# Two-layer diffusion backbone: mixer C's keys and values projected first, from tiles not yet divided by the rms

## The chip, the cores and the metric

One core of a Trainium2 chip runs the whole program in one launch. The metric is the device time of that launch in microseconds (us), from a few executions of the same program. The engines named below are TensorE (PE, with its weight loads PEld), VectorE (DVE), ScalarE (ACT), GpSimd (POOL) and SyncE (SP). They run side by side, each takes its own instructions in order, and they meet through semaphores.

## What is computed

One inference step of a two-layer network over 384 tokens (128 context tokens and 256 latent tokens), model width 1024. Layer 0 mixes with a state space model and gated DeltaNet; layer 1 mixes with two kinds of attention (C and D). Each layer ends with a feed-forward block with a short convolution. The part that matters here is the entry of layer 1:

```python
h = _modulate(x, norm1_g, sh1, sc1)        # rms-norm, times g * (1 + sc1), plus sh1
proj = h @ w_in_cd                         # 1024 -> 2304 columns
qc, kc, vc, qd, kd, vd = split(proj)       # 512, 128, 128, 512, 512, 512
qc = _rms(qc per head of 64, c_qn); kc = _rms(kc per head, c_kn)
qd = _rms(qd per head, d_qn);       kd = _rms(kd per head, d_kn)
# latent tokens: q and k are rotated (rope2d); then attention C and D, output projection
x = x + g1 * out
x = x + g2 * ffn(_modulate(x, norm2_g, sh2, sc2))
```

Context tokens use one pair of shift and scale vectors, latent tokens another. `_rms(v, g)` is `v / sqrt(mean(v^2) + 1e-6) * g`.

## The kernel before

**Layout.** The residual stream `x` lies in 8 tiles of 128 features x 384 tokens. Every projection works in a split format: an operand is a high part (`ah` of an activation, `wh` of a weight) and a low part (`al`, `wl`), each of a reduced-precision 32-bit type, and a product is three matmuls: low x high, high x low, high x high. In layer 1's input projection (`block`) the activation tile is the stationary operand (128 features x 128 tokens, three chunks c of tokens), and the weights move (512 or 256 columns). A block of 512 columns is 8 features tiles x 3 chunks x 3 products = 72 matmuls into three PSUM banks.

**Weights.** `load_unit` (L266) brings 512 KB: SP loads the raw weights, ACT rounds them to `wh`. In layer 1 (`self.added`) ACT also writes the raw weights, negated and rounded, into `wl`, and POOL issues a second DMA that adds the raw weights onto them in SBUF (L277), so that the rest stays. There are four buffers for `wh` and `wl` and three for the raw tile. `w_in_cd` is 18 units in the order in which `block` takes them: queries of C (4 units of 512 columns), keys and values of C (2 units of 256 columns), then keys, queries and values of D (4 units each). The first four are preloaded.

**Entry of layer 1** (`layer_cd`, L1339). `norm_stats` (L1036) squares the 8 tiles on ACT, adds them on DVE, sums over features with matmuls against a column of ones (L1051), makes the reciprocal root r on DVE (`rsqrt`, 11 small instructions) and broadcasts r over the partitions with three more matmuls (L1059). `norm_mod` (L1063) then multiplies each tile by gain and r on DVE (L1077), adds the shift on ACT and rounds (`ah`, L1080), and takes the rest on DVE (`al`, L1081). `raw_mod` (L1086) is the variant of the feed-forward block: it makes the two parts from `x` times gain alone, without r and without the shift; there the shifts ride along as two more columns and r is multiplied in afterwards.

**PSUM.** In layer 1 there are three banks `mm` for a projection, two `sc`, two `pt` and one `po`. A new block needs each `mm` bank emptied by DVE (times the head gain, L1375) and ACT (square, L1377; for values a copy, L1425). The `ah` and `al` tiles have eight buffers each, so a ninth pair takes the place of the first.

**Order of the work.** The program text gives the dependences; the order in which each engine gets its instructions is made by a planner (`Order`, L1618). It gives every instruction a duration, follows the dependences, and lets each engine take, among what is ready, the instruction with the longest path behind it. A changed program is therefore planned anew as a whole.

Of the kernel before, what the change touches and what calls it, by code (L numbers as in the profile page):

```python
# [12 lines left out]
F32 = mybir.dt.float32  # L13
F32R = mybir.dt.float32r
I32 = mybir.dt.int32
AF = mybir.ActivationFunctionType
ALU = mybir.AluOpType
# [4 lines left out]
P = 128  # L22
D = 1024
KD = D // P
NCTX = 128
NLAT = 256
T = NCTX + NLAT
EPS = 1e-6
# [19 lines left out]
def _offsets(table):  # L48
# [14 lines left out]
    ("o16", 128), ("o32", 128), ("o64", 128), ("par", 8), ("npar", 8), ("ind", 16), ("dinit", 32),  # L63
    ("wm0", 128), ("wm1", 128), ("rcos", 2 * 32), ("rsin", 2 * 32),
]
# [14 lines left out]
def _consts():  # L80
    c = {}
    i = np.arange(P)
# [29 lines left out]
    c["wm0"] = np.where(i[None, :] <= i[:, None], 0.0, -1e30)  # L112
    c["wm1"] = np.where(i[:, None] <= i[None, :], 0.0, -1e30)
    comb = np.zeros((P, 8))
    for r in range(32):
# [27 lines left out]
def prep(inp):  # L143
# [50 lines left out]
    units = []  # L194
    for at, width in ((0, 512), (512, 256), (1280, 512), (768, 512), (1792, 512)):
        kk = 1024 // width
        blk = wc[:, at:at + width].reshape(KD // kk, kk, P, width).transpose(0, 2, 1, 3)
        units.append(blk.reshape(KD // kk, P, 1024))
# [18 lines left out]
class Trunk:  # L217
# [818 lines left out]
    def norm_stats(self, pool, tag="aux"):  # L1036
# [12 lines left out]
        for part in (sum_, sq):  # L1049
            for c in range(3):  # L1050
                nc.tensor.matmul(pss[:, c:c + 1], part[:, P * c:P * c + P], self.c("one"),  # L1051
                                 start=part is sum_ and c == 0, stop=part is sq and c == 2)
        ms = t(pool, [P, 3], "nms")
        v.tensor_scalar(ms, pss, 1.0 / D, EPS, ALU.mult, ALU.add)
        r = t(pool, [P, 3], "nr")
        self.rsqrt(pool, r, ms, "nrs")
# [28 lines left out]

    def raw_mod(self, pool, l, which):  # L1086

# [3 lines left out]
        part = 3 * which  # L1091
# [5 lines left out]
        for k in range(KD):  # L1097
            a, b = t(self.ap, [P, T + 2], "ah", F32R), t(self.ap, [P, T + 2], "al", F32R)
            sh = self.mod[l][:, 8 * part + k, :]
            nc.scalar.copy(a[:, T:], sh)  # L1100
            v.tensor_sub(b[:, T:], sh, a[:, T:].bitcast(F32))
            for c, s, e in SEGS:
                nc.scalar.mul(a[:, s:e], self.x[k][:, s:e], gs[:, k, c:c + 1])
                v.scalar_tensor_tensor(b[:, s:e], self.x[k][:, s:e], gs[:, k, c:c + 1], a[:, s:e].bitcast(F32),  # L1104
                                       ALU.mult, ALU.subtract)
            hh.append(a)
            hl.append(b)
# [231 lines left out]
    def layer_cd(self):  # L1339
# [3 lines left out]
        with tc.tile_pool(name="dpl", bufs=1, reuse_waits="tile") as pool:  # L1343
            pre = self.preload([I["w_in_cd"][n] for n in range(4)])
            hh, hl = self.norm_mod(pool, 1, 0, self.norm_stats(self.np, "pt"))
            ck, cv_ = t(pool, [P, P], "cck"), t(pool, [P, P], "ccv")
# [3 lines left out]
            lam = self.lambdas(pool)  # L1350
            nu = [0]

            def block(width):
# [14 lines left out]

            def normed(ps, nh, gain, tag):

                out = t(pool, [P, 3, nh, 64], tag)
                ss = t(pool, [P, 3, nh], "ass")
                for c in range(3):
# [4 lines left out]
                    v.tensor_reduce(ss[:, c], sq.rearrange("p (h d) -> p h d", d=64), AX.X, ALU.add)  # L1378
                v.tensor_scalar(ss, ss, 1.0 / 64, EPS, ALU.mult, ALU.add)
                r = t(pool, [P, 3, nh], "asr")  # L1380
# [35 lines left out]
            flat = lambda x: (lambda c: x[:, c].rearrange("p h d -> p (h d)"))  # L1416

            pq = block(512)
            qc = normed(pq, 8, self.s("cqn"), "aqc")
            qcT = to_features(flat(qc), 4, "aqT")  # L1420
            pkv = block(256)
            kc = normed(pkv, 2, self.s("ckn"), "akc")
            vc = t(pool, [P, 3, P], "avc")
            for c in range(3):
                nc.scalar.copy(vc[:, c, :], pkv[c][:, 128:256])  # L1425
            nc.sync.dma_start(self.O["new_ck"], kc[:, 0].rearrange("p h d -> p (h d)"))
# [519 lines left out]
```

## Time and profile before

| what | value |
|---|---|
| time, median of 3 runs | 1172.72 us (1171.16 to 1173.33) |
| the profiled execution's own time | 1167.5 us |
| its span, first to last instruction | 1165.7 us |
| PE busy | 1114.2 us, 96% of the span |
| DVE, ACT, POOL busy | 804.1, 607.0, 25.5 us |
| mean granted TensorE clock | 0.977 of full speed |
| feed-forward block 0 ends on PE | 683.6 us into the span |
| input projection of keys of D begins | 720.9 us |

The span leaves out what lies before the first and after the last instruction. Busy shares are means over stages with different limits; a stage is read from its own stretch. "Granted clock" 1.00 is 2.4 GHz, 0.50 is 1.2 GHz. PE rows give the start of an instruction and its time through the array; neighbours overlap, so the pace is the distance of their starts.

### The profile page before, as it was taken

What the parts mean: (1) busy time and instruction counts of PE and PEld (TensorE: products, weight loads), DVE (VectorE), ACT (ScalarE), POOL (GpSimd) and SP (SyncE); (2) the same over time, 40 slices, a digit from 0 to 9 for tenths busy, and PEclk for the clock granted to TensorE, in tenths of its full rate; (3) what the DMA queues carried; (4) which work ended last, traced back from release to release, by engine and by line L of the source; (5) the groups of instructions that cost most, each with busy time, mean ns of one, the idle gap of its engine ahead of it and who ended that gap; (6) DMA issues with size and microseconds to landing.
All of it is one profiled execution on the core that took longest, in us unless ns stands there. A gap on an engine that the chain in (4) does not pass through costs nothing.

```text
span 1165.7 us, 20343 instructions
## 1 busy us (share of the span) xinstructions
PE 1114.2 (96%) x7699; PEld 968.6 (83%) x7699; DVE 804.1 (69%) x2071; ACT 607.0 (52%) x1327; POOL 25.5 (2%) x41
## 2 busy tenths in 40 slices
PE   4899999999999999999999989999999999999998
PEld 1587676686558999999999978667699999999998
DVE  7987688789876868767753447574867877676332
ACT  5666364557545555555542346755655655554221
POOL 0000000000000000000000011011000000000000
PEclk8688998999999999999999989999999999999999
DMA  9343465446864233433334479666253343333541
GB/s 376 138 121 134 150 226 173 157 144 246 333 236 132 95 110 126 141 113 127 121 117 133 125 180 235 147 154 135 56 109 127 111 142 109 127 130 101 159 137 53
DMA packets 54482, 174.49 MB, mean 150 GB/s; under 512 B 8688, under 2 KB 12656, under 8 KB 54128
## 3 DMA queue, kind: packets, MB, share of 16 engines
q1 hardware_dynamic: 49200, 154.72, 39.5%
q0 software_dynamic: 3744, 13.63, 7.1%
q10 hardware_dynamic: 1440, 4.85, 1.1%
q8 instruction: 60, 0.98, 0.3%
q14 instruction: 38, 0.31, 0.1%
HBM read 170.16 MB, written 3.01 MB: 149 GB/s over the span
## 4 chain that ended last, share of the span: by engine, by line
PE 85%; DVE 7%; ACT 3%; DMA 2%; issue 1%; ACTq 0%; SPq 0%; DVEq 0%
PE mm L1127 16%; PE mm L1128 16%; PE mm L1126 16%; PE mod L1011 3%; PE mm L1364 2%; PE mm L1366 2%; PE mm L1365 2%; PE pj L1128 1%; PE sc L1486 1%; PE pj L1127 1%; PE pj L1126 1%; DVE xt L1158 1%; PE mq L1011 1%; PE mod L1126 1%; PE mod L1128 1%
## 5 line engine op out<-in xcount | busy, mean ns | idle before, releaser
L274 ACT CAST wh<-raw 128x1024 fp32r<-128x1024 f32 (+2 forms) x193 | 194.1, 1027 | 198.8 <-PE mm L1128 160.9
L279 DVE TENSOR_TENSOR wl<-raw,wh 128x1024 fp32r<-128x1024 f32 x167 | 195.5, 1191 | 109.3 <-ACT wh L274 109.3
L1126 PE MATMUL mm<-ah,wl 128*128 128x386 f32 (+1 forms) x732 | 234.0, 342 | 3.5 <-DVE xt L1158 2.0
L1127 PE MATMUL mm<-al,wh 128*128 128x386 f32 (+1 forms) x732 | 232.9, 340 | 1.9 <-DVE al L1104 1.4
L1128 PE MATMUL mm<-ah,wh 128*128 128x386 f32 (+1 forms) x732 | 232.7, 340 | 0.0
L1126 PEld LDWEIGHTS mm<-ah,wl 128*128 128x128 f32 x732 | 137.5, 190 | 5.4 <-issue 2.4
L1127 PEld LDWEIGHTS mm<-al,wh 128*128 128x128 f32 x732 | 137.6, 190 | 3.0 <-DVE al L1104 2.1
L1128 PEld LDWEIGHTS mm<-ah,wh 128*128 128x128 f32 x732 | 137.8, 190 | 0.0
L1128 PE MATMUL mm<-fgh,wh 128*128 128x384 f32 x352 | 107.2, 339 | 0.0
L1127 PE MATMUL mm<-fgl,wh 128*128 128x384 f32 x352 | 106.9, 338 | 0.0
L1126 PE MATMUL mm<-fgh,wl 128*128 128x384 f32 x352 | 106.8, 338 | 0.0
L1185 ACT ACTIVATE fz<-fz,fsh 128x128 f32<-128x128 f32 x88 | 35.6, 450 | 67.2 <-DVE fz L1182 67.2
L1126 PEld LDWEIGHTS mm<-fgh,wl 128*128 128x128 f32 x352 | 65.3, 188 | 0.0
L1127 PEld LDWEIGHTS mm<-fgl,wh 128*128 128x128 f32 x352 | 65.2, 188 | 0.0
L1128 PEld LDWEIGHTS mm<-fgh,wh 128*128 128x128 f32 x352 | 65.1, 188 | 0.0
L1158 DVE SCALAR_TENSOR_TENSOR xt<-mm,mod,xt 128x128 f32<-128x128 f32 (+1 forms) x38 | 14.1, 413 | 62.5 <-PE mm L1128 62.5
L1182 DVE TENSOR_TENSOR fz<-mm,nrb 128x384 f32<-128x384 f32 x88 | 45.9, 550 | 0.2
L1190 DVE SCALAR_TENSOR_TENSOR fy<-fz,sml,fy 128x127 f32<-128x127 f32 x88 | 36.4, 414 | 12.9 <-ACT fy L1188 12.1
L276 ACT ACTIVATE wl<-raw 128x1024 fp32r<-128x1024 f32 x26 | 27.5, 1059 | 28.2 <-PE mm L1365 22.7
L1126 PE MATMUL pj<-ah,wl 128*128 128x384 f32 x112 | 39.9, 358 | 2.1 <-DVE wl L279 2.1
L1197 DVE SCALAR_TENSOR_TENSOR fs<-fz,fsh,fs 128x128 f32<-128x128 f32 x88 | 32.7, 414 | 12.5 <-ACT fs L1195 11.2
L1128 PE MATMUL pj<-ah,wh 128*128 128x384 f32 x112 | 40.8, 364 | 0.0
(664 smaller groups left out, 2220.5 us busy)
## 6 DMA issues: line engine op xcount, KB each, us to landing
raw<-in_ffn_up_dram SPq DMA_DIRECT2D x88, 512.0 KB, 3.4
raw<-in_w_mod_dram SPq DMA_DIRECT2D x54, 512.0 KB, 4.7
raw<-in_ffn_down_dram SPq DMA_DIRECT2D x32, 512.0 KB, 4.4
wh<-in_w_mod_dram SPq DMA_DIRECT2D x21, 512.0 KB, 6.0
wl<-in_w_mod_dram SPq DMA_DIRECT2D x21, 512.0 KB, 6.1
raw<-in_w_in_ab_dram SPq DMA_DIRECT2D x20, 512.0 KB, 3.5
raw<-in_w_in_cd_dram SPq DMA_DIRECT2D x18, 512.0 KB, 5.6
wl<-in_w_in_cd_dram POOLq DMA_DIRECT2D x18, 512.0 KB, 7.1
```

Source lines behind the costliest of these rows:

```text
L274: nc.scalar.copy(wh[:, :cols], raw[:, :cols])
L276: nc.scalar.mul(wl[:, :cols], raw[:, :cols], -1.0)
L279: nc.vector.tensor_sub(wl[:, :cols], raw[:, :cols], wh[:, :cols].bitcast(F32))
L1011: nc.tensor.matmul(pr[32 * n:32 * n + 32], self.sc[:, k, 30 - 2 * b:62 - 2 * b], raws[n // 2][:, 512 * (n % 2):512 * (n % 2) + 512], start ...
L1126: nc.tensor.matmul(out, wl, xh, start=first, stop=False)
L1127: nc.tensor.matmul(out, wh, xl, start=False, stop=False)
L1128: nc.tensor.matmul(out, wh, xh, start=False, stop=last)
L1158: self.nc.vector.scalar_tensor_tensor(self.x[n][:, s:e], ps[:, s:e], self.m(l, gate, n, c), self.x[n][:, s:e], ALU.mult, ALU.add)
L1182: v.tensor_mul(z[i][0], ps[:, 0:T], rb)
L1185: nc.scalar.activation(pa[:, a:b], pa[:, a:b], AF.Identity, bias=sa[:, c:c + 1])
L1190: v.scalar_tensor_tensor(y[:, a + 1:b], pa[:, a:b - 1], w[:, 0:1], y[:, a + 1:b], ALU.mult, ALU.add)
L1197: v.scalar_tensor_tensor(s[:, a:b], pb[:, a:b], sb[:, c:c + 1], s[:, a:b], ALU.add, ALU.mult)
```

## The change

Keys and values of C become the first block of the input projection, and it no longer works on the normalised tiles. `raw_mod` makes tiles that hold `x` times gain only. Since the rms is one number per token, the projected rows are the wanted ones times the rms, except for the shift's part. That part is a row per token group: shift (two columns) times the same weights gives two rows, which are added as rms x row by one small product per token chunk. The keys are normalised per head, so the common factor drops out once the epsilon is scaled by the mean square; the values are multiplied by r. The other four blocks use normalised tiles as before. The weight units are stored in the new order.

```diff
-    ("wm0", 128), ("wm1", 128), ("rcos", 2 * 32), ("rsin", 2 * 32),
+    ("cond", 2), ("wm0", 128), ("wm1", 128), ("rcos", 2 * 32), ("rsin", 2 * 32),
...
+    c["cond"] = (i[:, None] % 32) == np.arange(2)[None, :]
...
-    for at, width in ((0, 512), (512, 256), (1280, 512), (768, 512), (1792, 512)):
+    for at, width in ((512, 256), (0, 512), (1280, 512), (768, 512), (1792, 512)):
...
-    def raw_mod(self, pool, l, which):
+    def raw_mod(self, pool, l, which, n=T + 2):
...
-            a, b = t(self.ap, [P, T + 2], "ah", F32R), t(self.ap, [P, T + 2], "al", F32R)
-            sh = self.mod[l][:, 8 * part + k, :]
-            nc.scalar.copy(a[:, T:], sh)
-            v.tensor_sub(b[:, T:], sh, a[:, T:].bitcast(F32))
+            a, b = t(self.ap, [P, n], "ah", F32R), t(self.ap, [P, n], "al", F32R)
+            if n > T:
+                sh = self.mod[l][:, 8 * part + k, :]
+                nc.scalar.copy(a[:, T:], sh)
+                v.tensor_sub(b[:, T:], sh, a[:, T:].bitcast(F32))
...
             pre = self.preload([I["w_in_cd"][n] for n in range(4)])
-            hh, hl = self.norm_mod(pool, 1, 0, self.norm_stats(self.np, "pt"))
+            raw = self.raw_mod(self.np, 1, 0, T)
+            sh, sl_ = t(pool, [P, KD, 2], "ash", F32R), t(pool, [P, KD, 2], "asl", F32R)
+            nc.scalar.copy(sh, self.mod[1][:, 0:KD, :])
+            v.tensor_sub(sl_, self.mod[1][:, 0:KD, :], sh.bitcast(F32))
+            norm = self.norm_stats(self.np, "pt")
+            rms, inv = t(pool, [P, 3], "arms"), self.r
+            v.tensor_mul(rms, self.ms, inv)
+            eps = t(pool, [P, 3], "aeps")
+            v.tensor_scalar(eps, self.ms, EPS, None, ALU.mult)
+            hh, hl = self.norm_mod(pool, 1, 0, norm)
...
+            def raw_block():
+                (rh, rl), width, kk = raw, 256, 4
+                ps = [self.mm([P, width]) for _ in range(3)]
+                pw = self.bank("po", [2, width])
+                for u in range(2):
+                    wh, wl = pre[u]
+                    for c in range(3):
+                        for i in range(kk):
+                            k = kk * u + i
+                            sl, ts_ = slice(width * i, width * i + width), slice(P * c, P * c + P)
+                            nc.tensor.matmul(ps[c], rl[k][:, ts_], wh[:, sl], start=k == 0, stop=False)
+                            nc.tensor.matmul(ps[c], rh[k][:, ts_], wh[:, sl], start=False, stop=False)
+                            nc.tensor.matmul(ps[c], rh[k][:, ts_], wl[:, sl], start=False, stop=False)
+                    for i in range(kk):
+                        sl = slice(width * i, width * i + width)
+                        k = kk * u + i
+                        self.mm3(pw, (sh[:, k], sl_[:, k]), (wh[:, sl], wl[:, sl]), k == 0, k == KD - 1)
+                nu[0] = 2
+                rows = t(pool, [2, width], "art4")
+                nc.scalar.copy(rows, pw)
+                pr = self.bank("pt", [2, 3, P])
+                for c in range(3):
+                    nc.tensor.matmul(pr[:, c, :], rms[:, c:c + 1].to_broadcast([P, 2]), ident, start=True, stop=True)
+                each = t(pool, [2, 3, P], "ado", bufs=2)
+                nc.scalar.mul(each[:, 0], pr[:, 0], self.c("cond")[0:2, 0:1])
+                nc.scalar.mul(each[:, 1:], pr[:, 1:], self.c("cond")[0:2, 1:2])
+                for c in range(3):
+                    nc.tensor.matmul(ps[c], each[:, c, :], rows, start=False, stop=True)
+                return ps
...
-                v.tensor_scalar(ss, ss, 1.0 / 64, EPS, ALU.mult, ALU.add)
+                if eps is None:
+                    v.tensor_scalar(ss, ss, 1.0 / 64, EPS, ALU.mult, ALU.add)
+                else:
+                    v.scalar_tensor_tensor(ss, ss, 1.0 / 64, eps.unsqueeze(2).to_broadcast([P, 3, nh]),
+                                           ALU.mult, ALU.add)
...
+            pkv = raw_block()
+            kc = normed(pkv, 2, self.s("ckn"), "akc", eps)
+            vc = t(pool, [P, 3, P], "avc")
+            for c in range(3):
+                nc.scalar.mul(vc[:, c, :], pkv[c][:, 128:256], inv[:, c:c + 1])
             pq = block(512)
             qc = normed(pq, 8, self.s("cqn"), "aqc")
             qcT = to_features(flat(qc), 4, "aqT")
-            pkv = block(256)
-            kc = normed(pkv, 2, self.s("ckn"), "akc")
-            vc = t(pool, [P, 3, P], "avc")
-            for c in range(3):
-                nc.scalar.copy(vc[:, c, :], pkv[c][:, 128:256])
```

## Rows read from the trace of the kernel before

**Rows 1.** The page's first part: busy time, share and instructions of each engine.

```profile
PE 1114.2 (96%) x7699; PEld 968.6 (83%) x7699; DVE 804.1 (69%) x2071; ACT 607.0 (52%) x1327; POOL 25.5 (2%) x41
```

**Rows 2.** Windows from 600 us: length, busy us per engine, clock, DMA share, GB/s.

```profile
core 0: us, PE busy (x) PEld busy (x) DVE busy (x) ACT busy (x) POOL busy (x), PEclk, DMA share, GB/s
600.00:676.00 76.00, 76.00 (x435) 76.00 (x434) 30.20 (x43) 23.16 (x29) 0.31 (x1) 1.00 0.43 134
684.00:688.00 4.00, 1.50 (x12) 1.42 (x12) 3.83 (x27) 4.00 (x6) 1.73 (x2) 1.00 0.40 70
688.00:692.00 4.00, 1.62 (x6) 1.36 (x6) 1.58 (x12) 2.53 (x4) 0.86 (x1) 0.61 1.04 211
692.00:696.00 4.00, 3.63 (x9) 2.59 (x10) 3.36 (x10) 1.61 (x4) 0.00 (x0) 0.54 1.02 289
696.00:700.00 4.00, 4.00 (x19) 3.27 (x18) 2.53 (x9) 3.04 (x6) 0.86 (x1) 1.00 1.05 323
700.00:720.00 20.00, 19.71 (x122) 17.38 (x120) 13.92 (x41) 13.46 (x20) 3.46 (x4) 1.00 0.97 226
720.00:884.00 164.00, 158.88 (x823) 115.71 (x824) 112.40 (x418) 101.50 (x237) 14.71 (x17) 1.00 0.56 129
```

**Rows 3.** Timeline of PE, 683 to 721 us: start, us, what, idle before and releaser.

```profile
683.41 0.33 PE L1128 MATMUL mm<-fgh,wh 128*128 128x384 f32 x1
685.18 0.83 PE L1051 MATMUL pt<-cst,nacc 128*128 128x1 f32 x6 [1.43 <-DVE nacc L1047]
...
689.49 1.62 PE L1059 MATMUL pt<-cst,nr 128*128 128x128 f32 x6 [2.81 <-DVE nr L294]
692.37 0.80 PE L1364 MATMUL mm<-wh,al 128*128 128x512 f32 x1 [1.26 <-DVE al L1081]
...
709.38 0.63 PE L1364 MATMUL mm<-wh,al 128*128 128x512 f32 x2
709.84 0.63 PE L1365 MATMUL mm<-wl,ah 128*128 128x512 f32 x2
...
710.78 0.28 PE L1364 MATMUL mm<-wh,al 128*128 128x256 f32 x1
...
719.33 0.38 PE L1410 MATMUL pt<-cst,aqc 128*128 128x128 f32 x2
720.89 0.74 PE L1364 MATMUL mm<-wh,al 128*128 128x512 f32 x2 [1.18 <-ACT avc L1425]
```

**Rows 4.** Timeline of PE at 114 us: 16-column stationary beside a full one.

```profile
114.52 0.34 PE L1126 MATMUL su<-ah,wl 128*16 128x384 f32 x1
114.69 0.34 PE L1126 MATMUL pj<-ah,wl 128*128 128x384 f32 x1
```

**Rows 5.** Timeline of PE: plain f32 products, 128 columns, then 256 columns, in pairs.

```profile
46.03 0.94 PE L1059 MATMUL sy<-cst,nr 128*128 128x128 f32 x6
...
747.12 1.08 PE L1509 MATMUL po<-acpt,avc 128*64 128x256 f32 x6
```

**Rows 6.** Raw tiles of feed-forward 1, by line: min/median/max ns, first and last start.

```profile
L1103 ACT ACTIVATE ah<-xt,ngs x16: 387/448/504, 872.5 to 881.3; 128x128 fp32r<-128x128 f32 x8, 128x256 fp32r<-128x256 f32 x8
L1104 DVE SCALAR_TENSOR_TENSOR al<-xt,ngs,ah x16: 349/421/492, 880.0 to 885.2; 128x128 fp32r<-128x128 f32 x8, 128x256 fp32r<-128x256 f32 x8
```

**Rows 7.** Timeline of DVE at 683 us: the last residual addition.

```profile
683.78 0.74 DVE L1158 SCALAR_TENSOR_TENSOR xt<-mm,mod,xt 128x128 f32<-128x128 f32 x2
```

**Rows 8.** Timeline of ACT, then of POOL: the second weight unit's low part.

```profile
683.52 0.53 ACT L1042 ACTIVATE nsq<-xt 128x384 f32<-128x384 f32 x1 [7.21 <-DVE xt L1158]
683.95 1.04 ACT L276 ACTIVATE wl<-raw 128x1024 fp32r<-128x1024 f32 x1
...
685.30 0.87 POOL L277 DMA_DIRECT2D wl<-in_w_in_cd_dram  x1 [8.60 <-DVE lmp L1454]
```

**Rows 9.** POOL's DMA issues at 675, 685 and 689 us: us to landing.

```profile
wl<-in_w_in_cd_dram POOLq DMA_DIRECT2D x1, 512.0 KB, 7.2
...
wl<-in_w_in_cd_dram POOLq DMA_DIRECT2D x1, 512.0 KB, 5.3
...
wl<-in_w_in_cd_dram POOLq DMA_DIRECT2D x1, 512.0 KB, 11.4
```

More of the change, by code (lines that the diff above doesn't have):

```diff
@@ L1052, in norm_stats @@
                                  start=part is sum_ and c == 0, stop=part is sq and c == 2)
-        ms = t(pool, [P, 3], "nms")
+        self.ms = ms = t(pool, [P, 3], "nms")
         v.tensor_scalar(ms, pss, 1.0 / D, EPS, ALU.mult, ALU.add)
-        r = t(pool, [P, 3], "nr")
+        self.r = r = t(pool, [P, 3], "nr")
         self.rsqrt(pool, r, ms, "nrs")
@@ L1367, in block, with normed @@
                 return ps
-            def normed(ps, nh, gain, tag):
+            def normed(ps, nh, gain, tag, eps=None):
                 out = t(pool, [P, 3, nh, 64], tag)
```

## Prediction

> **What bounds the kernel now.** I read the page's busy times first: PE is busy for 1114 of 1166 us, and no other engine comes near [rows 1]. So time can be won where PE stands still or runs slowly, and every matmul that is added costs its own time unless it falls into such a hole. Then I went through windows of the layer that the change touches. Before 684 us PE is full and DVE and ACT have more than half their time free; from 684 to 692 us PE works 3.1 of 8 us, and from 688 to 696 the granted clock is 0.61 and 0.54, so most of the time at the lower of its two levels, 1.2 GHz. From 696 us PE is full again at full clock, and from 720 to 884 us it lacks only 5.1 of 164 us [rows 2]. The hole at the entry of layer 1 is the only large one here.
>
> The timeline of PE gives its parts [rows 3]. The feed-forward block's last product starts at 683.41 us; at the pace of 0.18 us that stretch is over at 683.59. Then PE waits 1.43 us for the sum of squares, 2.81 us for the reciprocal root, 1.26 us for the first normalised tile, and after the keys and values 1.18 us for ACT to empty a bank. The first block of D starts at 720.89 us: 37.3 us after the feed-forward block.
>
> What would those 37.3 us hold without waits, at full clock? The sums of squares take 1.5 us (685.18 to 686.68, where the next idle time of 2.81 us begins). The broadcast of r takes 0.94 us at full clock (the same six records at 46 us [rows 5]; here they took 1.62 [rows 3]). The query block is 72 products at 0.23 us (two starts lie 0.46 apart [rows 3]), 16.6 us; it took 692.37 to 710.78, 18.4 us, because it began at the low clock. Keys and values are 72 products from 710.78 to 719.33, 8.55 us, or 0.119 each. Two transposes take some 0.25 us. The sum is 27.8, so 9.5 us of the 37.3 are lost: 6.7 idle, 0.7 and 1.8 at the low clock, 0.3 in the draining of the array.
>
> **What is removed.** The block of keys and values needs r only at its end, so it can fill the time in which PE now waits for r. Its tiles come from x alone. Seven of the eight x tiles are final before the last residual additions; the eighth is final at 684.5 [rows 7]. A raw tile is two ACT products of about 0.45 us and two DVE ones of about 0.42 [rows 6]. Most of the 32 run under the feed-forward block, where DVE is busy for 30 and ACT for 23 of 76 us [rows 2]; I take that as free. Only the last two tiles fall behind 683.5 us, about 1.8 us on ACT and 1.7 on DVE, side by side; they are features 6 and 7, needed in the second half of the block, some 6 us later. Without that cover the 16 products of ACT would be 7.2 us in front of the block.
>
> **What is added on PE.** The two shift rows are 24 products of 256 moving columns with a stationary operand of two columns. No row here has two columns; the nearest has 16, and it takes its full 0.175 us of the stream like its 128-column neighbour [rows 4]. So each is priced like a full one, 24 x 0.119 = 2.85 us; a price of nothing would need them to run beside others, and the 16-column ones did not. The broadcast of rms is three plain f32 products of 128 columns, 0.94 us as for r [rows 5]. The three last products are plain f32, two rows deep and 256 columns wide: doubling the 128-column row gives 1.7 us, the 256-column row gives 1.0 for six records that ran in pairs; I take 1.3. Together 5.1 us, between 4.8 and 5.5. The small DVE steps (rms, epsilon, low part of the shift) are under 0.2 us each and lie before the root or beside it. The value products with r replace copies one for one.
>
> **The new sequence.** At 683.6 PE can start the first half of the raw block: its low weights were issued at 675 us and took 7.2 us [rows 9], so they are there by 683. This half is 36 x 0.119 = 4.3 us, its shift rows 1.4, the sums of squares 1.5: work until 690.8. The root is ready at 689.3 (the moment at which the broadcast starts now, less a hand-over), which adds two broadcasts, 1.9 us. The second half needs the second unit's low weights. ACT makes their negative at 683.95, behind a square that waits for x, POOL issues the addition at 685.30 [rows 8], and it took 5.3 us [rows 9]: 690.6. So in the existing times nothing is late. The normalised tiles then take the buffers of the raw ones as these are used up, and about 1.75 us each on DVE (four operations of 0.35 to 0.48 us) against 2.1 us in which PE uses one up: from 691 on they are ahead of the query block, which begins near 699.
>
> The sum on PE is 27.8 + 5.1 = 32.9 us instead of 37.3, a gain of 4.4, less what still waits. The query block takes the three banks of the keys and values, which ACT and DVE must empty, and the same hand-over costs 1.18 us today at the other end of the block [rows 3]. The change moves it and does not remove it. That leaves 3.2 us. Behind this, PE has nearly no idle time up to 884 us [rows 2], so an earlier start is passed on. The profiled execution's 1167.5 us become 1164.3; the median of the runs shown stands 5.2 us above that execution, and the same difference from it gives **1169.5 us**. A difference under 0.2% (2.3 us) could not be told from no change.
>
> **Rivals.**
>
> *A second wait at the bank hand-over.* ACT serves squares, value products, weight casts and normalised tiles in one row. It is busy for 24.6 us between 684 and 720 [rows 2]; the change adds some 2.5 us there and wants it done 3 to 4 us earlier, so about 27 of 32.5. If two weight operations of 1.04 us [rows 8] stand before the square that frees a bank, the hand-over costs 3.3 instead of 1.2 and the gain is 1.1: 1171.6, no measurable change. For it speaks that today's hand-over already waits for ACT; against it that the planner can put the square first.
>
> *The second unit's weights are late, and the clock falls.* The DMA engines are full from 688 us on, and the addition issued at 689 us took 11.4 us instead of 5.3 [rows 2, 9]. With that duration the second unit lands at 696.7. PE then runs out of work at 692.6, waits 4.1 us, and starts at the low clock again, which today costs the query block 1.8 us. The sum is 4.4 - 1.2 - 4.1 - 1.8, 2.7 us slower: 1175.4. With the clock's part it decides against the change from a landing near 694 us, 8.7 us after the issue. For it speaks that the buffer of that unit is freed only when the feed-forward block ends; against it that the unit is the first of three additions and took 5.3 us. The Trainium skill ("TensorE: Matmul & The Clock Gate", section "HAM oscillation — how this bites in real kernels") says the same against such loops: an array that waits for a transfer inside them falls back to half rate and pays it again at the restart. The trace agrees on the fall, with 0.61 and 0.54 after the waits here [rows 2]. Another page speaks for the change: "DMA: Bandwidth & Descriptors" (the Trainium skill, section "Anatomy of one DMA — SWDGE (gpsimd) path") fits such a DMA with 2.0 us plus its bytes at 436 GB/s, an estimate of 3.2 us for 512 KB, by which this rival would be out; no addition in these rows is that short, and the rows decide.
>
> *More is won.* The hand-over is hidden behind the three last products (0), and the plan behind it closes 1.5 of the 5.1 us that PE lacks later, since keys of C are ready before the queries: 5.9 us, 1166.8. Against it: nothing in the rows shows that those later gaps hang on the keys.
>
> **How the numbers follow.** The forecast gets 0.50, with a range of its own from 1168 to 1171.3; of this about 0.10 lies within 0.2%. The hand-over rival gets 0.25, the late weights 0.15, the larger gain 0.10. So faster 0.40 + 0.10 = 0.50, no change 0.10 + 0.25 = 0.35, slower 0.15. The range goes from the larger gain, 1166.5, to just short of the late weights, 1175. The new plan of the whole program can move any of these by a microsecond or so, which is why the forecast's own range is as wide as it is.
>
> **What would show it.** Right: in the changed profile PE goes from the feed-forward block into products on 256 columns without a pause, the clock row stays at 1.00 through 684 to 700 us, the 24 shift products take about 0.12 us each, and the first block of D begins some 33 to 35 us after the feed-forward block. Wrong: an idle time of PE before the raw block's second half with a low clock after it; the bank hand-over above 2 us; raw tiles that stand in front of the weight casts under the feed-forward block, so that PE is no longer full before 684 us; or a gain at the entry that the attention stages give back as new gaps behind 720 us.

## The result, and the profile after

| | median | lowest to highest | runs |
|---|---|---|---|
| before | 1171.82 us | 1165.74 to 1174.80 | 20 |
| changed | 1176.43 us | 1171.61 to 1186.91 | 20 |

The ratio is 1.0053, 95% interval [1.0038, 1.0067]: the change made the kernel slower by 0.53%; the medians lie 4.6 us apart. The forecast of 1169.5 us had the wrong sign, and the time lies 1.4 us above its range.

The page's first part, of the changed kernel, against [rows 1]:

```profile
PE 1125.3 (96%) x7735; PEld 976.7 (83%) x7735; DVE 810.2 (69%) x2091; ACT 613.3 (52%) x1347; POOL 25.4 (2%) x41
```

PE is busy for 11 us more, with 36 more instructions. That is more than the added products cost: the mean granted clock of the profiled execution fell from 0.977 to 0.972, and PE counts as busy at the lower clock too.

Single executions differ in places that the change does not touch: around 404 us, in the first feed-forward block, where PE has the same instructions in the same order in both kernels, the profiled execution of the changed kernel ran 4 us at a granted clock of 0.59 and that of before did not. So the traces are compared over one stage: from the start of the first feed-forward block's last product (683.41 us before [rows 3], 686.13 after) to the first product of the second one. This stage took 195.53 us before and 200.70 after. The 5.2 us are in it. Each kernel has one traced execution, so a stage is one execution's, while the medians are of 6 to 20 executions.

The timeline of PE at the entry of layer 1, changed kernel (start, us, what, idle before and releaser), against [rows 3]:

```profile
686.13 0.33 PE L1130 MATMUL mm<-fgh,wh 128*128 128x384 f32 x1
687.65 0.35 PE L1376 MATMUL mm<-wh,al 128*128 128x256 f32 x1 [1.19 <-DVE al L1106]
...
700.15 0.83 PE L1060 MATMUL pt<-cst,nr 128*128 128x128 f32 x6
700.91 0.82 PE L1389 MATMUL pt<-cst,arms 128*2 128x128 f32 x6
701.66 0.28 PE L1130 MATMUL po<-wh,ash 128*2 128x256 f32 x1
702.43 1.56 PE L1394 MATMUL mm<-art,ado 2*128 2x256 f32 x6 [0.49 <-ACT art L1385]
704.84 0.62 PE L1408 MATMUL mm<-wh,al 128*128 128x512 f32 x1 [0.85 <-ACT avc L1470]
705.26 0.63 PE L1409 MATMUL mm<-wl,ah 128*128 128x512 f32 x1
```

The three long waits of before for the sum, the root and the first normalised tile (1.43, 2.81 and 1.26 us) are gone; 1.19, 0.49 and 0.85 us stand in their place. The last row is the new loss: a product of 512 columns starts 0.42 us after the one before, where the pace at full clock is 0.23. Windows of the changed kernel show the granted clock (last but two; columns as in [rows 2]):

```profile
688.00:704.00 16.00, 15.49 (x126) 13.57 (x124) 10.70 (x56) 9.15 (x16) 2.59 (x3) 1.00 0.99 259
704.00:706.00 2.00, 1.16 (x3) 0.96 (x4) 1.95 (x7) 1.98 (x7) 0.00 (x0) 0.77 1.00 188
706.00:708.00 2.00, 2.00 (x6) 1.52 (x6) 2.00 (x8) 1.33 (x4) 0.00 (x0) 0.50 0.97 292
708.00:710.00 2.00, 2.00 (x10) 1.61 (x9) 1.93 (x9) 0.80 (x2) 0.00 (x0) 0.88 0.11 34
...
744.00:746.00 2.00, 0.66 (x4) 0.54 (x5) 1.04 (x4) 1.99 (x5) 0.67 (x1) 1.00 0.56 104
746.00:748.00 2.00, 2.00 (x6) 1.16 (x5) 1.46 (x4) 2.00 (x8) 0.00 (x0) 0.51 1.02 180
748.00:750.00 2.00, 2.00 (x8) 1.49 (x7) 0.95 (x4) 0.77 (x3) 0.00 (x0) 0.64 0.84 240
```

As forecast the clock is 1.00 through the raw block. But it falls twice behind it, at the start of the query block and at 746 us. Summed over windows of 2 us, what the clock lacks to 1.00, times the length, is 3.4 us in this stage, and it was 3.4 before. The fall at the entry was not removed; it was moved and split.

The second fall lies where attention C begins. PE there, changed kernel:

```profile
738.10 0.82 PE L1458 MATMUL pt<-cst,aqc 128*128 128x128 f32 x6
...
739.93 0.49 PE L1458 MATMUL pt<-cst,akc 128*128 128x128 f32 x3
...
741.63 0.49 PE L1534 MATMUL sc<-akT,aqT 64*128 64x128 f32 x2
742.04 0.96 PE L1410 MATMUL mm<-wh,ah 128*128 128x512 f32 x3
742.93 0.48 PE L1534 MATMUL sc<-akS,aqT 64*128 64x128 f32 x2
745.34 0.48 PE L1534 MATMUL sc<-akT,aqT 64*128 64x128 f32 x2 [1.92 <-ACT acp L1547]
745.84 0.63 PE L1408 MATMUL mm<-wh,al 128*128 128x512 f32 x1
```

The keys of C, projected first, are transposed at 739.93, behind the last of the four query transposes. Their last rows were ready long before, as DVE shows:

```profile
722.00 0.22 DVE L1449 TENSOR_TENSOR akc<-art,art 128x64 f32<-128x64 f32 x1
```

The first scores follow at 741.63, 55.5 us into the stage against 48.7 before. D's key block, the work with which PE bridges such waits, begins 0.4 us earlier than before. So at the first score 69 of its 72 products have started, where before it were 41: three are left (742.04), then PE stands for 1.92 us and the clock falls. In the kernel before, the same wait of the scores for ACT is 0.41 us:

```profile
732.14 0.48 PE L1486 MATMUL sc<-akT,aqT 64*128 64x128 f32 x2
...
735.75 0.48 PE L1486 MATMUL sc<-akT,aqT 64*128 64x128 f32 x2 [0.41 <-ACT acp L1499]
```

TensorE's time in the stage, summed over starts by kind of product, divides the 5.2 us. Added products: 5.28 (shift 1.10, 0.94 and 0.93; broadcast of rms 0.75; last products 1.56). Idle time above 60 ns: 10.06 to 7.44, so -2.61. Broadcast of r, now at full clock: -0.86. The 512-column products: +1.57. Score products on half the array in C and D: +1.90. The sum is 5.3.

Of the 1.90, 0.31 is the low clock at 748 us. The other 1.59 comes from which score products the plan puts next to each other (a plain f32 product is two records). The last two of D, one for each half of the array, stand together before, and the next product starts 0.85 us after the first; after the change other work stands between them, and each takes 0.84 us. Before, then after:

```profile
850.42 0.92 PE L1546 MATMUL mm<-akdT,aqT 64*128 64x384 f32 x4
851.27 0.61 PE L1126 MATMUL sc<-ah,wl 128*128 128x384 f32 x2
...
856.08 0.91 PE L1594 MATMUL mm<-akdT,aqT 64*128 64x384 f32 x2
...
858.45 0.91 PE L1594 MATMUL mm<-akdT,aqT 64*128 64x384 f32 x2
```

That is 0.83 us. Two products of C on 384 columns stood together in the same way before (749.02 to 749.90) and do not after: 0.76 us.

### The profile page after: what moved, and what is told of

Same layout as the page of the kernel before. It is cut to its first block, busy times and chain, and to the rows that moved or that the text cites. A ratio compares the mean times of both kernels' runs of the same rounds, so it can differ in the third digit from the quotient of the medians.

```text
span 1174.6 us, 20451 instructions
## 1 busy us (share of the span) xinstructions
PE 1125.3 (96%) x7735; PEld 976.7 (83%) x7735; DVE 810.2 (69%) x2091; ACT 613.3 (52%) x1347; POOL 25.4 (2%) x41
## 4 chain that ended last, share of the span: by engine, by line
PE 87%; DVE 6%; ACT 3%; DMA 2%; issue 1%; ACTq 0%; SPq 0%; DVEq 0%
PE mm L1129 16%; PE mm L1130 16%; PE mm L1128 16%; PE mod L1012 3%; PE mm L1408 2%; PE mm L1409 2%; PE mm L1410 2%; PE sc L1534 1%; PE pj L1130 1%; PE pj L1129 1%; PE pj L1128 1%; PE mod L1128 1%; PE mm L1594 1%; PE mod L1130 1%; PE mod L1129 1%
## 5 line engine op out<-in xcount | busy, mean ns | idle before, releaser
L1130 PE MATMUL mm<-fgh,wh 128*128 128x384 f32 x352 | 103.5, 336 | 0.0
L1129 PE MATMUL mm<-fgl,wh 128*128 128x384 f32 x352 | 103.5, 336 | 0.0
L1128 PE MATMUL mm<-fgh,wl 128*128 128x384 f32 x352 | 103.2, 336 | 0.0
```

What stands on the lines that cost most here:

```text
L1128: nc.tensor.matmul(out, wl, xh, start=first, stop=False)
L1129: nc.tensor.matmul(out, wh, xl, start=False, stop=False)
L1130: nc.tensor.matmul(out, wh, xh, start=False, stop=last)
```

## The experiments

Each run is timed against before on its own chip (medians 1171.0 to 1171.8 us). The marks are starts on PE in the traced execution, in us into the stage.

| kernel | query block | D's keys | C's first scores | stage | median | ratio to before, interval |
|---|---|---|---|---|---|---|
| before | 8.95 | 37.48 | 48.73 | 195.53 | | |
| changed | 18.70 | 37.07 | 55.49 | 200.70 | 1176.43 | 1.0053 [1.0038, 1.0067] |
| order only | 23.94 | 40.69 | 59.29 | 207.68 | 1181.83 | 1.0112 [1.0076, 1.0148] |
| order, keys turned first | 23.97 | 41.05 | 55.61 | 200.41 | 1175.89 | 1.0030 [1.0015, 1.0046] |
| no shift | 14.12 | 33.28 | 51.63 | 196.84 | 1170.71 | 0.9999 [0.9983, 1.0016] |
| x in eight tiles | 18.30 | 36.92 | 55.60 | 201.35 | 1176.26 | 1.0050 [1.0025, 1.0075] |
| wide | 18.80 | 35.57 | 54.00 | 197.68 | 1173.83 | 1.0031 [1.0006, 1.0056] |
| shift alone wide | 18.90 | 37.28 | 55.98 | 201.19 | 1175.20 | 1.0033 [1.0014, 1.0052] |
| keys turned first | 18.71 | 37.16 | 51.72 | 196.51 | 1169.64 | 0.9989 [0.9972, 1.0006] |
| keys first, wide | 18.80 | 35.94 | 50.50 | 195.31 | 1170.51 | 1.0000 [0.9981, 1.0019] |
| keys first, wide, eight tiles | 18.33 | 35.47 | 50.03 | 195.41 | 1170.03 | 0.9990 [0.9973, 1.0006] |
| keys first, wide, four rows | 17.60 | 35.08 | 49.64 | 194.48 | 1167.45 | 0.9970 [0.9948, 0.9991] |
| turned block | 13.80 | 38.42 | 58.96 | 212.24 | 1179.26 | 1.0078 [1.0043, 1.0114] |
| turned, eight tiles, keys first | 15.38 | 38.59 | 55.22 | 201.41 | 1174.81 | 1.0036 [1.0021, 1.0052] |

**The order alone, on normalised tiles.**

```diff
-    for at, width in ((0, 512), (512, 256), (1280, 512), (768, 512), (1792, 512)):
+    for at, width in ((512, 256), (0, 512), (1280, 512), (768, 512), (1792, 512)):
...
+            pkv = block(256)
+            kc = normed(pkv, 2, self.s("ckn"), "akc")
...
             pq = block(512)
...
-            pkv = block(256)
...
```

> Only the order is changed: keys and values of C come first, but on normalised tiles, with no shift rows and no rms products. The stage is taken from the start of the last product of feed-forward 0 to the first of feed-forward 1: 195.5 us in the kernel before, 200.7 in the changed one. Theory A (the loss is the sum of 5.3 us of added products, two falls of the clock and a later start of attention C, against a hole that is only partly filled): order alone keeps the whole hole at the entry and adds the later start of attention C, some 2 to 3.5 us: stage 197.5 to 199. Theory B (the order alone makes the loss, since the long chain of the queries now starts last, and the added products lie in the hole): stage 200 or more, as slow as the changed kernel. If the order costs nothing, 195.5.

It lost 12 us in the stage: in theory B's range, and 7 us above the changed kernel. Its timeline of PE:

```profile
690.25 1.62 PE L1059 MATMUL pt<-cst,nr 128*128 128x128 f32 x6 [2.66 <-DVE nr L294]
693.13 0.58 PE L1364 MATMUL mm<-wh,al 128*128 128x256 f32 x1 [1.26 <-DVE al L1081]
...
694.58 0.79 PE L1364 MATMUL mm<-wh,al 128*128 128x256 f32 x2 [0.45 <-DVE al L1081]
```

and windows of it:

```profile
692.30:696.30 4.00, 2.72 (x11) 2.43 (x12) 2.94 (x9) 2.00 (x5) 0.00 (x0) 0.50 1.04 188
696.30:700.30 4.00, 4.00 (x21) 4.00 (x21) 3.37 (x11) 1.60 (x4) 0.00 (x0) 0.53 1.00 281
```

The entry's waits stay. The block behind them is half as wide and waits for four more tiles (0.45, then 1.25, 0.37 and 0.39 us), and the clock stays at 0.50 for longer than before [rows 2]. In this order the raw tiles are worth 7.0 us of the stage (207.68 to 200.70), and the new order takes more than that away.

**Without the shift.** This kernel leaves the shift out of C's keys and values: no shift products, no rms broadcast, no last products.

> The changed kernel without the shift's part of keys and values: the 24 two-column products, the broadcast of rms and the three two-row products are left out, so the keys and values lack the shift. Theory A: these products cost what they take on PE, 5.3 us, and if they also bring the fall of the clock at the query block, 1.8 us more: stage 195.4, or 193.6 with the clock. Theory B (they lie in the hole): stage within 1 us of 200.7.

3.9 of the 5.3 us came back. In front of the query block PE now waits longer:

```profile
699.37 0.47 PE L1392 MATMUL mm<-wh,al 128*128 128x512 f32 x1 [1.89 <-ACT avc L1454]
```

and the clock falls there (0.74, 0.50) and at the scores, as in the change. PE's idle time in the stage is 1.4 us longer than in the changed kernel: that part of the added work had lain in waits. So the added work alone doesn't explain the loss: without it the kernel only comes level with before.

**x in eight tiles.** The planner keeps an engine's reads of a tile behind that engine's own last write to it. DVE writes the residuals, so with x in one tile the low parts (DVE, L1106) all follow the last residual; ACT, which only reads x, makes its parts from 612 us on. DVE in the changed kernel shows it:

```profile
686.50 0.74 DVE L1160 SCALAR_TENSOR_TENSOR xt<-mm,mod,xt 128x128 f32<-128x128 f32 x2 [3.50 <-PE mm L1130]
687.16 0.74 DVE L1106 SCALAR_TENSOR_TENSOR al<-xt,ngs,ah 128x128 fp32r<-128x128 f32 x2
```

```diff
-    def load_x(self, pool):
+    def load_x(self, pool, apart=False):
+        if apart:
+            self.x = [self.t(pool, [P, T], f"xt{k}") for k in range(KD)]
...
```

> The changed kernel with the residual stream in eight tiles of their own instead of one, so that the planner may place the low parts of the raw tiles on DVE before the last residual addition. Theory E (the first raw product waits 1.2 us because the planner keeps all DVE reads of the one tile behind its last DVE write): the low parts of features 0 to 5 run under feed-forward 0, the wait of 1.2 us goes, the root of the rms comes some 3 us earlier, and the stage is 1.2 to 2 us shorter, 198.7 to 199.5; the same at the entry of feed-forward 1 takes another 1 to 2 us. Rival: the low parts stay late for another reason, stage 200.7.

The raw block starts at once in the trace of this run, and that is all:

```profile
680.63 0.34 PE L1130 MATMUL mm<-fgh,wh 128*128 128x384 f32 x1
680.81 0.40 PE L1381 MATMUL mm<-wh,al 128*128 128x256 f32 x2
681.89 0.36 PE L1381 MATMUL mm<-wh,al 128*128 128x256 f32 x1 [0.69 <-DVE xt L1160]
```

A wait of 0.69 us comes one step later, the query block starts 0.4 us earlier, and the stage is no shorter. This wait is real and not the cause.

**Wide operands.** The same number of products, with 128 stationary columns or rows in place of two, by slices of 128 columns of the shift tile and zero rows.

```diff
-                pw = self.bank("po", [2, width])
+                pw = self.bank("po", [P, width])
...
-                        self.mm3(pw, (sh[:, k], sl_[:, k]), (wh[:, sl], wl[:, sl]), k == 0, k == KD - 1)
+                        at = slice(2 * k, 2 * k + P)
+                        self.mm3(pw, (sh[:, at], sl_[:, at]), (wh[:, sl], wl[:, sl]), k == 0, k == KD - 1)
...
-                rows = t(pool, [2, width], "art4")
+                rows = t(pool, [P, width], "art4")
...
-                    nc.tensor.matmul(pr[:, c, :], rms[:, c:c + 1].to_broadcast([P, 2]), ident, start=True, stop=True)
+                    nc.tensor.matmul(pr[:, c, :], rms[:, c:c + 1].to_broadcast([P, P]), ident, start=True, stop=True)
```

> The changed kernel, with the same number of products and the same columns streamed, but the shift products and the rms broadcast use a stationary operand of 128 columns, and the last three products are 128 rows deep (all rows but two are zero). Theory C (the clock falls at the start of the query block because PE just ran narrow products): the granted clock stays at 1.00 through the first 4 us of the query block, the block takes 16.6 us instead of 18.4, and the stage is 1.8 us shorter, 198.9. Rival D (the clock falls because of the two waits of 0.5 and 0.85 us around the last products): the clock falls as before, the block takes 18.4 us, stage 200.7.

The stage is 3.0 us shorter, with nearly the same waits: 0.60 and 0.87 us in front of the query block, 1.92 at the scores. Its windows there:

```profile
704.40:706.40 2.00, 1.13 (x6) 0.90 (x6) 1.88 (x7) 2.00 (x8) 0.00 (x0) 1.00 0.95 172
706.40:708.40 2.00, 2.00 (x10) 1.65 (x9) 2.00 (x8) 1.39 (x5) 0.00 (x0) 1.00 0.89 270
...
745.00:747.00 2.00, 2.00 (x10) 1.34 (x10) 1.76 (x6) 2.00 (x8) 0.00 (x0) 1.00 0.95 184
```

The clock holds at both places. At the query block this goes with the edit in every trace: it fell there in all four kernels with two-wide products at the end of the raw block (changed, eight tiles, shift alone wide, keys turned first) and in none of the four with 128 (wide, and the three wide ones below). Why the later fall goes too, 40 us behind the last edited product, no run tells: a wait of 1.92 us at the scores went with a fall in four traces (changed, order only, eight tiles, shift alone wide) and not in this one.

**The shift products alone wide**, to tell the shift products between the full ones from the two-wide work at the end of the raw block. Against the run with all of them wide:

```diff
...
-                rows = t(pool, [P, width], "art4")
-                nc.scalar.copy(rows, pw)
+                rows = t(pool, [2, width], "art4")
+                nc.scalar.copy(rows, pw[0:2])
...
-                    nc.tensor.matmul(pr[:, c, :], rms[:, c:c + 1].to_broadcast([P, P]), ident, start=True, stop=True)
+                    nc.tensor.matmul(pr[:, c, :], rms[:, c:c + 1].to_broadcast([P, 2]), ident, start=True, stop=True)
...
```

> The changed kernel with 128 columns in the 24 shift products alone; the rms broadcast has two columns and the three last products two rows, as in the change. It divides the gain of the run with all of them wide (stage 200.70 to 197.68 us). If the shift products, which stand between the full ones from 688 to 702 us, are what lets the clock fall, the query block starts at a granted clock of 1.00 and the stage is near 197.7 us. If it is the narrow work in the last 5 us before the block (two-row products and two-column broadcast, with the idle 0.5 and 0.85 us among them), the clock falls at 18 us of the stage as in the change, and the stage stays near 200.7 us.

The stage was 201.19 us and the clock fell as in the change. Windows from the query block on:

```profile
702.10:704.10 2.00, 1.15 (x5) 0.90 (x5) 1.86 (x7) 2.00 (x8) 0.00 (x0) 0.96 1.00 190
704.10:706.10 2.00, 2.00 (x6) 1.54 (x5) 2.00 (x8) 1.40 (x5) 0.00 (x0) 0.50 0.95 311
```

So it is the rms broadcast on two columns and the last products on two rows, between the two short waits, after which the clock falls. The median (1175.20) lies between the two other kernels', and the interval leaves it open with which it goes; the trace goes with the changed kernel.

**Keys turned first.** One statement moves, with the line that makes its argument: the transposes of C's keys are written ahead of the query block.

```diff
+            kf = lambda c: kc[:, c].rearrange("p h d -> p (h d)") if c < 3 else ck
+            kcT = to_features(kf, 1, "akT", cols=4)[0]
             pq = block(512)
             qc = normed(pq, 8, self.s("cqn"), "aqc")
             qcT = to_features(flat(qc), 4, "aqT")
...
-            kf = lambda c: kc[:, c].rearrange("p h d -> p (h d)") if c < 3 else ck
-            kcT = to_features(kf, 1, "akT", cols=4)[0]
```

> The changed kernel with the transposes of C's keys written ahead of the query block instead of behind the queries' transposes; nothing else differs. Theory F (attention C starts late because keys and queries come to it one after the other: four transposes of queries, then the keys' transpose, two copies, a weight operation and a table load on ACT, all behind the long query chain): the first score moves from 55.5 us behind the last product of feed-forward 0 to 52 to 53.5, the wait of 1.9 us at the first scores and the fall of the clock behind it shrink, and the stage of 200.7 us becomes 197 to 199. Rival: the queries' own chain sets the start, and the stage stays within 1 us of 200.7.

It is the largest effect of a single edit to the changed kernel, 4.2 us of the stage, and the time is that of before. PE in this run:

```profile
720.12 0.49 PE L1458 MATMUL pt<-cst,akc 128*128 128x128 f32 x3
...
735.03 0.37 PE L1534 MATMUL sc<-akT,aqT 64*128 64x128 f32 x1
735.04 0.37 PE L1534 MATMUL sc<-akS,aqT 64*128 64x128 f32 x1
735.25 0.27 PE L1534 MATMUL sc<-akT,aqT 64*128 64x128 f32 x1
735.25 0.27 PE L1534 MATMUL sc<-akS,aqT 64*128 64x128 f32 x1
...
738.34 0.49 PE L1534 MATMUL sc<-akT,aqT 64*128 64x128 f32 x2 [1.07 <-ACT acp L1547]
```

The keys are turned before D's block, the first scores come 3.8 us earlier (59 products of D's key block have started, not 69) and before the last query transposes, the wait is 1.07 in place of 1.92 us, and the second fall of the clock is gone (1.00 from 737 to 741). By kind of product the gain is 2.3 us in 512-column products, 0.9 in idle time and 0.9 in the scores. The fall at the query block stays (0.56 and 0.59 in the windows from 701.3 to 705.3).

**Order only, keys turned first.** The same statement moved in the kernel with normalised tiles.

> The kernel before with the order alone changed (keys and values of mixer C first, on normalised tiles, 1181.83 us) and, new, the transposes of mixer C's keys written ahead of the query block. Theory A (the keys' transposes stand behind the four query transposes in the ring of the transposes' banks, and that holds attention C's first scores back whichever tiles the keys come from): the first scores come some 4 us earlier than the 59.3 us behind the feed-forward block's last product, as they did with the raw tiles (55.49 to 51.72), and the time falls by about 4 us to 1178. The rival (the order costs only through the half clock while the key block waits for its tiles): first scores at 59 us and 1181 to 1182 us. In both the granted clock stays near 0.5 from 4 to 15 us of the stage.

The stage lost 7.3 us of its 12, the median 5.9: more than the 4 expected, since the later fall of the clock, at 64 us of the stage, and one in attention D went with it. The 0.50 clock between 6 and 14 us stayed. So the order costs by two routes: the keys' transposes behind the queries', and on normalised tiles the waits and the half clock of the narrower block. The raw tiles cure the second. With the keys turned first in both kernels they are worth 3.9 us of the stage (200.41 to 196.51), near the 3.2 that I had given the whole change.

**Both cures, and with eight tiles.**

> The changed kernel with the keys' transposes first and with 128 columns and 128 rows in place of two in the shift products, the rms broadcast and the last products; x stays one tile. Theory A and C apart (late first scores, and the clock that falls behind the two-wide products): the stage is 200.7 less 4.2 (keys first alone gave 196.5) less some 1.9 for the query block at full clock, 194.6 us, and the time about 1167.8, some 2.5 to 3.5 us under the kernel before. The rival (both cures take the same loss, at the first scores): 196.5 and 1169.6 us, no better than the keys first alone.

> The changed kernel with its own products kept, but in the three forms that touch the waits alone: full-width stationary operands (as e2), eight tiles (as e3), keys' transposes first (as e5). If the losses are separate, they add up: 200.7 less 3.0 (measured for the width), less 1 to 3 (keys), so a stage of 194.5 to 197, and a time within 0.2% of the kernel before. If the waits only move from one place to another, 198 or more.

The stages are 195.31, between the two theories (1.2 us gained of the 1.9), and 195.41, within the sum, with no window of either below full clock before the second feed-forward block, and as long as before's 195.53. The time of the first (1.0000) can't tell the 1.2 us by which its stage is shorter than with the keys turned first alone.

**Four rows.** High and low part of the shifts side by side in one stationary operand: 16 shift products in place of 24. Against the run with keys first and wide operands:

```diff
...
-                        self.mm3(pw, (sh[:, at], sl_[:, at]), (wh[:, sl], wl[:, sl]), k == 0, k == KD - 1)
+                        nc.tensor.matmul(pw, sh[:, at], wh[:, sl], start=k == 0, stop=False)
+                        nc.tensor.matmul(pw, sh[:, at], wl[:, sl], start=False, stop=k == KD - 1)
...
```

> As the run with keys first and 128 columns, and the high and the low part of the shifts stand side by side in one stationary operand (four rows of the sum count), so that a feature takes two shift products and not three: 16 in place of 24. If the added products cost what they take on TensorE (24 took 2.97 us in the changed kernel, so 8 are 0.99 us), the stage is 1.0 us shorter than with 24 of them. The rival (the shift products lie in time in which TensorE would wait for the next raw tile): no difference, within 0.3 us.

The stage fell by 0.83 us to 194.48: the 8 products cost nearly their full time, and were not hidden. This is the only version with an interval under 1 (0.9970 [0.9948, 0.9991]): it beats both kernels. Its median is 3.1 us under that of 24 products; 0.8 of them stand in the stage, and for the rest I have no cause beyond the spread of the runs. PE at its query block, which waits once:

```profile
699.79 1.56 PE L1398 MATMUL mm<-art,ado 128*128 128x256 f32 x6 [1.15 <-ACT ado L1395]
701.44 0.50 PE L1412 MATMUL mm<-wh,al 128*128 128x512 f32 x1
```

**The block turned round.** Weights stationary, tokens moving with the shifts as two more columns, and six transposes back; then the same with eight tiles and the keys turned first.

> Another form of the change: keys and values of C first and from undivided tiles, but with the weights as the stationary operand and the tokens moving, so that the shift rides as two more columns (as in the feed-forward block); the two results are multiplied by r, the shift added, and turned back with six transposes. In place of 5.3 us of added products there are 0.7 us of transposes. Theory A: the stage falls by some 4.5 us and by 1.8 more if the clock no longer falls at the query block: 194.4 to 196.2, and the time comes to that of the kernel before or 0.1% under it. Rival: the longer way of the keys (multiplication, shift, turning) makes a new wait, stage above 198.

> The form of e6 with the residual stream in eight tiles and the keys' transposes ahead of the query block. Theories A, E and F together: 1.2 us less at the first raw product, 1 to 3 us less at the start of attention C, 1 to 2 us less at the entry of feed-forward 1: stage 189 to 193 us, and a time 0.2 to 0.5% under the kernel before. If E and F fall, as e6.

Fewer products, and slower; both forecasts failed (stages of 212.24 and 201.41). The query block begins at 13.8 us and then, in both, waits for one normalised tile after the other. PE and DVE of the first of the two:

```profile
702.52 0.50 PE L1394 MATMUL mm<-wh,al 128*128 128x512 f32 x1 [1.36 <-DVE al L1082]
...
704.24 0.50 PE L1394 MATMUL mm<-wh,al 128*128 128x512 f32 x1 [0.75 <-DVE al L1082]
```

```profile
703.43 0.75 DVE L1082 SCALAR_TENSOR_TENSOR al<-nh,mod,ah 128x256 fp32r<-128x256 f32 x2 [0.32 <-ACT ah L1081]
704.10 0.73 DVE L1078 SCALAR_TENSOR_TENSOR nh<-xt,ngs,pt 128x256 f32<-128x256 f32 x2
705.15 0.75 DVE L1082 SCALAR_TENSOR_TENSOR al<-nh,mod,ah 128x256 fp32r<-128x256 f32 x2 [0.32 <-ACT ah L1081]
```

The next low part comes 1.72 us after the one before (703.43 to 705.15), and the products of one tile fill less: PE waits 0.75 us each time. In the profiled execution the clock also stayed low for 20 us at the scores:

```profile
749.80:769.80 20.00, 20.00 (x46) 10.15 (x45) 9.23 (x40) 7.57 (x24) 0.86 (x1) 0.51 0.39 86
```

This execution (1185.35 us) was above the median of its kernel (1179.26); whether the others have that long a fall isn't known.

## Why the prediction was wrong

**Right.** PE is the bound, and every added product costs. The shift products took 2.97 us (2.85 forecast), the broadcast 0.75 (0.94), the last products 1.56 (1.3): 5.28 against 5.1. That the sum came so close is in part luck, since the errors of the parts cancel; and the 1.7 us for a doubled 128-column row is 1.9 by the row as shown (twice 0.94). The bank hand-over, 1.18 before, is 0.85 and another 0.49, 1.3 together against 1.2. The second unit's weights were never late: PE is busy for 15.49 of 16 us from 688 to 704. Both waiting rivals are out.

**The raw tiles under the feed-forward block, "I take that as free".** Wrong for DVE's half. The cover was there, but a rule of the plan kept it from being used: none of the 16 low parts runs before the last residual. [rows 6] had shown it: in the second feed-forward block ACT's parts start at 872.5 and DVE's only at 880.0. I had read the durations of these rows and not their starts. It cost 1.2 us at the start; taken away, 0.4 came back at the query block.

**The query block at 16.6 us.** It took 18.4 again (704.84 to 723.2). I had counted 1.8 us at the low clock as won, since the wait in front of it was gone; the clock fell again behind the two-wide products and the waits of 0.49 and 0.85. With the 1.3 us by which the raw block starts later than forecast, this is why D's block begins 37.1 us into the stage and not at the forecast 33 to 35. The run with wide operands shows it: nearly the same waits, clock 1.00, and 35.57.

The Trainium skill ("TensorE: Matmul & The Clock Gate", section "A second HAM failure mode: psum-queue depth-cycling") reports short idle times between groups of products, from cycling through PSUM banks, that let the clock swing. Here the runs go both ways: waits of 0.60 and 0.87 us for banks and rows left the clock at 1.00 where the products around them were wide, and 0.45 to 0.49 and 0.85 us went with a fall to 0.50 where they were two wide. Waits of this length alone don't tell; the 1.89 us of the run without the shift went with a fall with no two-wide product in front.

**"An earlier start is passed on."** The step that set the sign. Of the 3.2 us that the entry was to win, 0.4 was left at D's block (37.48 to 37.07), and from there to the end of the stage 5.6 us were lost (158.05 to 163.63). I had taken the stages behind 720 us as full, therefore as indifferent to what comes first. But PE's fullness there rested on an order: before, keys followed queries, and the first scores came 11.3 us after D's key block had begun, with 31 of its 72 products left to fill waits. Afterwards the query chain comes last and the keys' transposes wait behind it in the ring of two `pt` banks, though ready 18 us earlier: 18.4 us after D's block, 3 products left, 1.92 us idle, a low clock. One moved statement gave back 4.3 of the 5.6 us behind D's block, with raw tiles, and the order-only kernel gained from it too. The 1.3 that remain lie within the 1.59 us of score products that no longer stand side by side, which turning the keys first didn't change; the forecast had no term for them. The prediction had named such a give-back as what would show it wrong, but gave it no chance; its rival "more is won" had even taken the early keys as a gain.

**What stays open.** Why the new plan lays the score products apart, and why the clock's second fall is gone with wide operands too, where its wait stayed.

## What to carry to other kernels

Where a block is moved ahead, follow its results to their first use: a result that is early gains nothing while a ring of buffers, or a rule on whole tiles, holds it behind the late ones, and the late chain now meets an engine whose filler is used up. Price a removed clock loss only together with what will then stand in front of the same products. And before calling work hidden, look at when the same operation starts in the trace, not only how long it takes.

## What the hardware showed unexpectedly

The granted clock of TensorE fell to 0.50 behind 4.7 us (700.15 to 704.84) in which PE waited for 0.49 and 0.85 us and worked for the rest, mostly on two-wide operands; with 128-wide ones and slightly longer waits it stayed at 1.00. In one execution PE stayed at the lower level, 1.2 GHz, for 20 us though it was busy for 20.00 of them, with full products, half-array scores and transposes in turn; at the entry of before it stayed there for some 7 us (4 us at 0.61 and 4 at 0.54 [rows 2]). Score products on the two halves of the array (`akT` and `akS`) ran side by side with the keys turned first, 0.01 us apart, two products (four records) in 0.49 us (735.03 to 735.52); on one half alone, a single product (two records) took 0.49 in the changed kernel (741.63). What it saves hangs on which products the plan puts next to each other.
